# Four modulation vectors summed on VectorE, ScalarE and GpSimd during the projections, and a state-space term added by transposes

## The chip, the cores and the metric

One core of a Trainium2 chip runs the whole kernel. The metric is the device time of that core in microseconds (us), as the median of several runs. TensorE (PE in the profile) multiplies, VectorE (DVE), ScalarE (ACT) and GpSimd (POOL) do the elementwise work, SyncE (SP) issues most of the DMA transfers. Each engine takes its own instructions in order and waits on semaphores for the others.

## What is computed

Two transformer blocks in a row on 512 latent tokens of 1024 channels, with 256 context tokens. Cut to what the change touches:

```python
def first_block(x, c, ctx, c_ctx, w_mod, b_mod, ...):
    m_lat = jnp.split((silu(c) @ w_mod + b_mod)[:, None, :], 6, axis=-1)   # six vectors of 1024
    m_ctx = jnp.split(silu(c_ctx) @ w_mod + b_mod, 6, axis=-1)
    h_lat = modulate(rmsnorm(x, norm1_g), m_lat[0], m_lat[1])              # first shift and scale
    mix_lat = token_mixers(h_lat, h_ctx, w_in, ...)                        # projections, then four mixers
    x = x + m_lat[2] * (mix_lat @ w_out)
    h_lat = modulate(rmsnorm(x, norm2_g), m_lat[3], m_lat[4])              # second shift and scale
    return x + m_lat[5] * expert_choice_ffn(h_lat, ...)                    # 16 experts

def second_block(x, c, ctx, c_ctx, w_mod, b_mod, ...):
    sh1, sc1, gt1, sh2, sc2, gt2 = jnp.split(silu(c) @ w_mod + b_mod, 6)
    # state-space branch: per chunk, y = (masked decay * C B^T) xs  +  decay * C state  +  d * xs
    x = x + gt1 * token_mixer(modulate_2(x, norm1_g, sh1, sc1), ...)
    return x + gt2 * conv_ffn(modulate_2(x, norm2_g, sh2, sc2), ...)
```

The vectors of the change are number 3 and 4 of each block's six, `m_lat[3]`, `m_lat[4]`, `sh2` and `sc2`: only their latent row is needed, and only behind the mixers.

## The kernel before, in words

The program is written as Python generators, one for each strand of work, which `weave` (L321), `beside` (L360) and `filled` interleave: the strand with the least progress goes next, and each `yield` says how much progress it made. What is so interleaved goes to a scheduler that fixes the order of each engine's instructions by the order of writing and by when operands are ready; buffers come from rings and arenas, so a load into a ring's buffer waits for the last reader of that buffer. The stages in order of time are these.

- **Input** (0 to 52 us). `a_in` (L601) sums the first shift and scale of block one and makes the modulated tokens.
- **Projections** (52 to 222 us). `g_proj` (L701) multiplies the tokens with eleven blocks of `w_in` of 256 columns. A block comes in two loads of half a megabyte on SP (`base<-in_cola`), is split by `wsplit` (L1948) into a high part (ScalarE, L1963) and a low part (VectorE or GpSimd in turn, L1964), one block ahead, and multiplied in three passes by `chan` or `tok` (`bank_mm`, 24 matmuls to an accumulator, four accumulators). ScalarE and VectorE in turn copy the accumulators out (`cp`, L425 and L427). `a_gates` (L860) is a chain of small instructions on VectorE in the middle of it.
- **Mixers** (222 to 670 us). `phase_a` (L1443) weaves `g_dn`, a recurrence of twelve chunks in two directions (names `dn`, `bank_dn`, `bank_dnr`), with `others`: first `g_ft` and `g_na`, and beside them `g_mods`; then `g_df` beside `g_wo`; then `g_mid`.
- **Modulation vectors.** `g_mods` (L652) makes ten vectors for later. Each comes in two halves of 512 columns; `mod_rows` (L510) loads a half's weights in four loads of half a megabyte (a ring of three buffers, `mods<-in_cola`) and multiplies them by a 32-column silu vector, eight matmuls that leave rows. `mod_bcast` spreads the rows over 128 partitions by one more matmul, `mod_cols` (L521) turns them into columns by four transposes (L528), and `mod_cols_pk` (L533) packs them by eight matmuls into `bigbank`.
- **Router and experts** (670 to 1700 us), `g_b0`, `g_b1`, `g_b`.
- **Second block** (1700 us to the end). `part_c` weaves the attention `c_att` with `c_ssd`, the state-space branch, and then runs the output projections and the feed-forward part. In `c_ssd`, for each of four groups of eight heads, `state` (two directions, four steps) adds the term of the states into `of`, four chunks of 128 tokens by 512 channels. Then, for 16 pairs of a head pair and a chunk, `weights` builds the decay weights `W` (six VectorE instructions L2426 to L2430, two ScalarE steps and one of GpSimd, in a ring of four) and `mixed` adds two products into the accumulator `bank_y` (one bank): `xs` times `W`, and `of` times the identity, each for two heads of 64 channels. `out` reads the bank when its four chunks are done.

Of the kernel before, what the change touches and what calls it, by code (L numbers as in the profile page):

```python
# [390 lines left out]
class KA:  # L391
# [141 lines left out]
    def mod_cols_pk(self, s, wdram, bi, j, ring, rows, out):  # L533
        nc = self.nc
        t = self.big().rearrange("p (k g r) -> p k g r", k=8, g=4)
        for h in range(2):
            r = rows()
            self.mod_rows(s, wdram, 2 * j + h, ring, r)
            for kt in range(8):
                self.mm(t[64 * h:64 * h + 64, kt].rearrange("p g r -> p (g r)"), r[:, kt::8], self.ident)  # L540
        nc.vector.tensor_reduce(out, t[:, :, :, 0:2].rearrange("p c g r -> p c r g"), AX.X, OP.add)
        nc.vector.tensor_add(out, out, self.col("b_mod_pk", 8 * bi, 8)[:, :, None].to_broadcast([128, 8, 2]))
# [109 lines left out]
    def g_mods(self, tag, n):  # L652
        nc, I = self.nc, self.I
        self.md = tag
        with self.pool("mods") as P:
# [3 lines left out]
            self.mod_bcast(s1, wm, I["b_mod"], 2, wr, rows, self.gt1_b.ap(), self.sel)  # L659
# [5 lines left out]
            yield 0.1  # L665
            self.mod_bcast(s1, wm, I["b_mod"], 5, wr, rows, self.gt2_b.ap(), self.sel)
            yield 0.1
            mc, a = self.m2c_b.ap(), self.ab2_b.ap()
            s2, wm = self.s2b.ap(), "w_mod_2"
            for i, j in enumerate((0, 1, 3, 4)):  # L670
                self.mod_cols(s2, wm, "b_mod_2", j, wr, rows, mc[:, i])
                yield 0.1
            for i, (m, r, n) in enumerate(((1, 0, "norm1_g_2"), (1, 1, "norm1_g_2"), (3, 0, "norm2_g_2"))):
                nc.vector.scalar_tensor_tensor(a[:, i], mc[:, m, :, r], 1.0, self.col(n, 0, 8), op0=OP.add, op1=OP.mult)
            for i, j in enumerate((2, 5)):
# [8 lines left out]
                yield 0.1  # L684
# [16 lines left out]
    def g_proj(self, P):  # L701
# [91 lines left out]
        for t in range(4):  # L793
            z = nv()
            self.cp(z, self.tok(w, t))
            if t == 0:
                left()
            nc.scalar.dma_start(vdv[:, t], z)
        yield 0.04
        for t in range(2):  # L800
            self.cp(vc[:, t], self.tok(w, t, False))
        w.done()
# [4 lines left out]
        for i in range(2):  # L807
            nc.scalar.mul(q[:, i].rearrange("p (i r c) -> p r i c", i=4, r=8), self.chan(w, 128 * i).rearrange("p (r i c) -> p r i c", i=4, r=8), 0.125)
            yield 0.03
        w.done()  # L810
        w = block()
        for i in range(2):
            self.cp(k[:, i], self.chan(w, 128 * i), "v")
            if i == 0:
                next(gates)
                self.abT_b.free()
            self.cp(kc[:, i], self.chan(w, 128 * i, False))
            yield 0.05
# [6 lines left out]
        for a in range(2):  # L825
            w = block()
            for t in range(4):
# [4 lines left out]
                for e in range(2):  # L832
# [3 lines left out]
                    (nc.gpsimd.tensor_sub if e == 0 else nc.gpsimd.tensor_add)(o[:, :, :, e], o[:, :, :, e], u)  # L836
                yield 0.015
            if a == 1:
                for t in range(2):
                    self.cp(kc[:, t].rearrange("p m d -> p (m d)"), self.tok(w, t, False))  # L840
                yield 0.03
            w.done()
        w = block()
        for t in range(2):
            self.cp(v[:, t], self.tok(w, t, False))
        yield 0.03
        for t in range(4):
            self.cp(v[:, 2 + t], self.tok(w, t))
        yield 0.06
        w.done()  # L850
        w = block()
        for i in range(2):
            self.cp(self.uT_b.ap()[:, i], self.chan(w, 128 * i))
            yield 0.03
        w.done()
        cr.free()
        cr2.free()
# [896 lines left out]
class Kern(KB):  # L1754
# [517 lines left out]
    def c_ssd(self, P):  # L2272
# [84 lines left out]
        for gr in range(4):  # L2357
# [76 lines left out]
            def mixed(k):  # L2434
                pr, c = k // 4, k % 4
                if c == 0:
                    ys[pr] = self.bank((128, 512), "y")
                yb, W, tk = ys[pr], Ws.pop(k), slice(128 * c, 128 * c + 128)
                for z in range(2):
                    for h in range(2):  # L2440
                        o = 128 * pr + 64 * h
                        self.mm(yb[64 * h:64 * h + 64, tk], (of if z else xs)[:, c, o:o + 64], self.ident if z else W[:, h], z == 0, z == 1)
# [338 lines left out]
```

## Time and profile before

| | before |
|---|---|
| median of 3 runs | 2982.91 us (2982.39 to 2989.98) |
| the profiled execution | 2982.76 us |
| its span in the profile | 2980.9 us |
| TensorE busy | 2770.4 us, 93% of the span |
| VectorE, ScalarE, GpSimd busy | 1334.9, 902.3, 625.7 us |
| DMA moved | 658.53 MB, mean 221 GB/s |

How to read the profile: "busy" is the time in which an engine has at least one instruction under way. TensorE's instructions overlap at their ends, so the time that one takes in a stream is the distance of two starts and not its duration; a float32 matmul leaves two records, a transpose one. Names are those of the program's buffers without their numbers: `l`, `a`, `ab` and `base` are arenas of the first block, `sp` the ring of split weights, `mix` and `c` those of the second block.

### The profile page before, as it was taken

The numbers are of one execution on the slowest core, as the hardware profiler recorded it, in microseconds if no ns is written. First come the engines' busy times: TensorE is split into PE (matmuls) and PEld (weight loads), VectorE is DVE, ScalarE is ACT, GpSimd is POOL, SyncE is SP. The second block draws the span as 40 slices with busy tenths as digits, with TensorE's granted clock in tenths as the row PEclk, the third lists the DMA queues.
The fourth block names the chain that finished last, engine by engine and source line by source line (L and its number), as shares of the span: only waits on it lengthen the run. The fifth ranks groups of instructions, "written<-read, shape, count | busy, mean of one in ns | idle before, by whom it ended". The sixth has DMA issues, their size and how long they took to land.

```text
span 2980.9 us, 41808 instructions
## 1 busy us (share of the span) xinstructions
PE 2770.4 (93%) x16824; PEld 1776.0 (60%) x16824; DVE 1334.9 (45%) x2654; ACT 902.3 (30%) x1836; POOL 625.7 (21%) x660
## 2 busy tenths in 40 slices
PE   7999989997999999988888789999999899999998
PEld 4894547765334333332222267777777688888886
DVE  5522445655121211111101167878787854454445
ACT  5511225532111010100000044545454543343333
POOL 3121224531000000000000024232323322332222
PEclk9999999998999999999999999999999999999999
DMA  6216661038999999989999923324242464242331
GB/s 268 75 34 200 209 218 32 30 121 309 397 430 430 429 429 430 429 371 430 431 431 430 387 88 105 118 64 123 72 120 74 134 232 160 94 154 95 97 99 57
DMA packets 213122, 658.53 MB, mean 221 GB/s; under 512 B 13816, under 2 KB 131192, under 8 KB 188352
## 3 DMA queue, kind: packets, MB, share of 16 engines
q1 hardware_dynamic: 185504, 601.73, 52.4%
q10 hardware_dynamic: 26272, 49.93, 4.7%
q0 software_dynamic: 1152, 4.19, 0.3%
q8 instruction: 133, 2.18, 0.3%
q14 instruction: 61, 0.50, 0.1%
HBM read 632.07 MB, written 23.73 MB: 220 GB/s over the span
## 4 chain that ended last, share of the span: by engine, by line
PE 68%; DMA 16%; DVE 10%; issue 2%; ACT 2%; POOL 2%; SPq 1%; ACTq 0%; POOLq 0%; DVEq 0%
PE bank_mm L399 29%; PE bigbank L399 20%; DMA l<-in_w_up 6%; PE bank_pj L399 6%; DMA l<-in_w_down 4%; PE bank_c L399 4%; PE bank_dn L399 2%; DMA mods<-in_cola 2%; DMA l<-in_w_gate 1%; PE bank_sm L399 1%; DVE base L2426 1%; DVE mix L2430 1%; PE bank_dnr L399 1%; DVE mix L2429 1%; PE bank_mm L2181 1%
## 5 line engine op out<-in xcount | busy, mean ns | idle before, releaser
L399 PE MATMUL bank_pj<-c,c 128*128 128x512 f32 (+2 forms) x1368 | 319.7, 376 | 0.3 <-DVE c L1964 0.3
L399 PE MATMUL bank_mm<-c,c 128*128 128x512 f32 (+1 forms) x1608 | 304.4, 347 | 4.9 <-ACT b L1987 3.2
L399 PEld LDWEIGHTS bank_mm<-c,c 128*128 128x128 f32 x1608 | 259.3, 191 | 44.2 <-ACT b L1987 3.6
L399 PE MATMUL bigbank<-l 128*64 128x512 f32 (+1 forms) x1104 | 266.1, 594 | 17.9 <-DMA l<-in_w_up 13.1
L399 PEld LDWEIGHTS bank_pj<-c,c 128*128 128x128 f32 (+1 forms) x1368 | 225.7, 189 | 50.7 <-issue 17.5
L1963 ACT CAST c<-base 128x1024 fp32r<-128x1024 f32 x147 | 152.8, 1045 | 254.3 <-PE bigbank L399 105.7
L1964 POOL TENSOR_TENSOR c<-base,c 128x1024 fp32r<-128x1024 f32 x47 | 116.7, 2483 | 472.9 <-ACT c L1963 404.6
L1964 DVE TENSOR_TENSOR c<-base,c 128x1024 fp32r<-128x1024 f32 x100 | 136.3, 1365 | 136.8 <-ACT c L1963 133.7
L399 PEld LDWEIGHTS bigbank<-l 128*64 128x64 f32 (+1 forms) x1104 | 80.9, 141 | 175.8 <-issue 140.4
L1692 DVE TENSOR_TENSOR b<-l,bigbank 128x512 f32<-128x512 f32 x32 | 20.5, 683 | 340.8 <-PE bigbank L399 293.5
L1691 ACT ACTIVATE l<-bigbank 128x512 f32<-128x512 f32 x32 | 17.4, 595 | 423.7 <-PE bigbank L399 423.7
L399 PE MATMUL bank_mm<-l 128*64 128x512 f32 (+2 forms) x528 | 124.8, 601 | 9.1 <-DMA l<-in_w_down 8.0
L399 PE MATMUL bigbank<-out,c 128*128 128x512 f32 x480 | 113.8, 397 | 1.9 <-ACT out L2524 1.8
L399 PE MATMUL bank_c<-b 128*128 128x256 f32 (+3 forms) x496 | 110.0, 373 | 1.9 <-ACT b L425 0.8
L399 PE MATMUL bank_mm<-h,sp 128*128 128x512 f32 (+3 forms) x544 | 105.5, 382 | 4.3 <-ACT h L644 3.8
L399 PEld LDWEIGHTS bank_dn<-dn 64*64 64x64 f32 x1920 | 74.8, 134 | 55.0 <-issue 39.3
L399 PEld LDWEIGHTS bigbank<-out,c 128*128 128x128 f32 x480 | 91.7, 192 | 23.0 <-ACT out L2524 2.2
L399 PE MATMUL bigbank<-b,l 128*64 128x512 f32 x352 | 84.9, 614 | 21.8 <-DMA b<-in_w_up 10.9
L1717 DVE TENSOR_TENSOR b<-bank_mm,ab 64x512 f32<-64x512 f32 x16 | 10.9, 683 | 208.1 <-PE bank_mm L399 208.1
L1786 ACT ACTIVATE b<-bank_c,base 128x256 f32<-128x256 f32 x20 | 11.3, 563 | 304.6 <-PE bank_c L399 304.6
L399 PEld LDWEIGHTS bank_c<-b 128*128 128x128 f32 (+1 forms) x496 | 80.4, 188 | 37.2 <-issue 23.9
L399 PE MATMUL bigbank<-c,ffn 128*128 128x512 f32 x432 | 100.3, 390 | 0.0
(538 smaller groups left out, 5060.7 us busy)
## 6 DMA issues: line engine op xcount, KB each, us to landing
l<-in_w_up SPq DMA_DIRECT2D x36, 2048.0 KB, 14.6
l<-in_w_down SPq DMA_DIRECT2D x31, 2048.0 KB, 17.0
l<-in_w_gate SPq DMA_DIRECT2D x29, 2048.0 KB, 18.2
mods<-in_cola SPq DMA_DIRECT2D x80, 512.0 KB, 4.9
base<-in_w_in SPq DMA_DIRECT2D x68, 512.0 KB, 3.7
b<-in_w_gate SPq DMA_DIRECT2D x15, 2048.0 KB, 34.0
base<-in_w_gate SPq DMA_DIRECT2D x13, 2048.0 KB, 16.9
wo<-in_w_up SPq DMA_DIRECT2D x13, 2048.0 KB, 33.8
```

What stands on the lines that cost most here:

```text
L399: self.mm_ins = self.nc.tensor.matmul(out, l, r, start=start, stop=stop).ins
L1691: nc.scalar.activation(s, ac[0][:, j], AF.Silu)
L1692: nc.vector.tensor_mul(hid[:, 512 * j:512 * j + 512], s, ac[1][:, j])
L1717: nc.vector.tensor_mul(Y[pp, 0:512], dn[0:64], gt2[0:64, 0:512])
L1786: nc.scalar.activation(y, b, AF.Identity, scale=wc(1), bias=self.col(bname, i))
L1963: nc.scalar.copy(hi, raw)
L1964: (nc.vector if self.wn % 4 in self.losplit else nc.gpsimd).tensor_sub(lo, raw, hi.bitcast(F32))
L2181: nc.tensor.transpose(tb[:, z], p[:, 128 * (g0 + z):128 * (g0 + z) + 128], self.ident)
L2426: nc.vector.scalar_tensor_tensor(E[:, h], rw[:, h, 0], gc(1, 0, h), E[:, h], op0=OP.subtract, op1=OP.min)
L2429: nc.vector.tensor_scalar(W[:, h], cb[:, c, 0], gc(0, 0, h), None, op0=OP.mult)
L2430: nc.vector.scalar_tensor_tensor(W[:, h], cb[:, c, 1], gc(0, 1, h), W[:, h], op0=OP.mult, op1=OP.add)
```

## The change

Three things change.

1. `g_mods` makes six vectors where it made ten. The four that are left out, number 3 and 4 of both blocks, are made by the new `g_late_mods` inside `g_proj`, from the block behind the recurrence's query projections on to the last. Each half's weights now come in eight loads of a quarter megabyte (a ring of four buffers); VectorE (five of eight), ScalarE (three of eight, added by GpSimd) multiply them by the silu value of their partition and add up, and GpSimd adds the two sums (`mod_sums`). One half later TensorE sums over the partitions by matmuls with one moving column of ones (`mod_close`: eight of 64 columns for the packed form, four of 128 for the other), and VectorE adds the bias.
2. In `g_mods` the `yield` values change from a tenth to a sixth, so that the six vectors spread over the same stretch.
3. In `mixed` the product of `of` with the identity, two for each chunk, gives way to four transposes of 128 by 128 for each head pair, written into `bank_y` in front of the first product.

```diff
-    def mod_cols_pk(self, s, wdram, bi, j, ring, rows, out):
-        ...
+    def mod_sums(self, s, wdram, j, rings):
+        nc, (wr, da, pa, pp) = self.nc, rings
+        wv = self.block(wdram, j)
+        d, o = da(), pa()
+        for kt in range(8):
+            w, c = wr(), s[:, kt, 0:1]
+            self.ld(w, wv[:, kt])
+            if kt == 0:
+                nc.vector.tensor_scalar(d, w, c, None, op0=OP.mult)
+            elif kt in (1, 3, 6):
+                z = o if kt == 1 else pp()
+                nc.scalar.activation(z, w, AF.Copy, scale=c)
+                if kt > 1:
+                    nc.gpsimd.tensor_add(o, o, z)
+            else:
+                nc.vector.scalar_tensor_tensor(d, w, c, d, op0=OP.mult, op1=OP.add)
+            if kt == 3:
+                yield
+        nc.gpsimd.tensor_add(o, o, d)
+        self.msum = o
+
+    def mod_close(self, o, h, bias, out, pk):
+        p, n = (slice(64 * h, 64 * h + 64), slice(0, 8)) if pk else (slice(0, 128), slice(4 * h, 4 * h + 4))
+        t = self.bank((128, 8), "md")
+        for c in range(8 if pk else 4):
+            self.mm(t[p, n.start + c:n.start + c + 1], o[:, c::8] if pk else o[:, c * 128:(c + 1) * 128], self.km("one", 1))
+        self.nc.vector.tensor_add(out[p, n], t[p, n], bias[p, n])
+
+    def g_late_mods(self, P):
+        ...
+        of = [Ring(P, [512], 2, more=[Buf(self.M, [512]) for _ in range(2)])] + [Ring(self.M, [512], n) for n in (1, 2, 1)]
+        ...
+            for h in range(2):
+                yield from self.mod_sums(s, w, 2 * j + h, of)
+                if owed:
+                    owed.pop()()
+                owed.append(lambda o=self.msum, h=h, n=n, name=name, out=out, pk=pk: self.mod_close(o, h, self.col(name, n, 8), out, pk))
+                yield
+        owed.pop()()
@@ g_mods
-            self.mod_cols_pk(s1, wm, 0, 3, wr, rows, mp[:, 0])
-            yield 0.1
-            self.mod_cols_pk(s1, wm, 1, 4, wr, rows, mp[:, 1])
-            for i, j in enumerate((0, 1, 3, 4)):
-                self.mod_cols(s2, wm, "b_mod_2", j, wr, rows, mc[:, i])
-                yield 0.1
+            for j in range(2):
+                self.mod_cols(s2, wm, "b_mod_2", j, wr, rows, mc[:, j])
+                yield 1 / 6
@@ g_proj, at some 16 places from the block of the values on
+            if t % 2 == 0:
+                next(sums)
@@ c_ssd, mixed
                 if c == 0:
-                    ys[pr] = self.bank((128, 512), "y")
+                    b = ys[pr] = self.bank((128, 512), "y")
+                    for z in range(4):
+                        nc.tensor.matmul(b[:, 128 * z:128 * z + 128], of[:, z, 128 * pr:128 * pr + 128], self.ident, start=z == 0, stop=False, is_transpose=True)
-                for z in range(2):
-                    for h in range(2):
-                        o = 128 * pr + 64 * h
-                        self.mm(yb[64 * h:64 * h + 64, tk], (of if z else xs)[:, c, o:o + 64], self.ident if z else W[:, h], z == 0, z == 1)
+                for h in range(2):
+                    o = 128 * pr + 64 * h
+                    self.mm(yb[64 * h:64 * h + 64, tk], xs[:, c, o:o + 64], W[:, h], False, c == 3)
```

Where instructions stand in an engine's row, before and after, is told by the built programs. SP's row in the projections of the kernel before, from the weights of the first blocks (`base_95`) to the first loads of the mixers (`dn` and `mods`):

```order
L430 DMA base_95<-in_cola 128x1024 x4
L430 DMA ab_138<-in_b_mod 128x1024
L430 DMA ab_139<-in_b_mod 128x1024
L430 DMA base_95<-in_cola 128x1024 x16
L430 DMA dn_1853<-in_k_ct 128x2x512 x2
L430 DMA mods_1951<-in_cola 128x1024
```

The same of the kernel after; the loads of the sums are those of 128x512 into `sp_920`, `sp_921` and two pieces of `l_105`:

```order
L430 DMA base_95<-in_cola 128x1024 x10
L430 DMA l_105<-in_cola 128x512 x2
L430 DMA sp_921<-in_cola 128x512
L430 DMA l_105<-in_cola 128x512
L430 DMA sp_920<-in_cola 128x512
L430 DMA l_105<-in_cola 128x512
L430 DMA base_95<-in_cola 128x1024
L430 DMA l_105<-in_cola 128x512 x2
```

Sixteen weight loads in a row have become ten, and the last six stand one by one among the loads of the sums.

VectorE's row of the kernel before, in the block of the values and at the head of the chain of `a_gates` (L874 on); L427 copies an accumulator out and L1964 is a low part of split weights:

```order
L427 COPY sp_888<-bank_mm 128x256
L1964 TENSOR_TENSOR sp_353<-base_95,sp_349 128x1024
L427 COPY l_105<-bank_mm 128x256
L874 TENSOR_TENSOR l_105<-bank_mm,ab_123 128x48
L587 SCALAR_TENSOR_TENSOR l_105<-l_105 128x48
```

And of the kernel after, where the same lines are L2013 (split), L923 and L624 (`a_gates`), and L541 and L548 are the sums:

```order
L541 TENSOR_SCALAR l_105<-l_105,ab_126 128x512
L548 SCALAR_TENSOR_TENSOR l_105<-sp_920,ab_126,l_105 128x512
L2013 TENSOR_TENSOR sp_353<-base_95,sp_349 128x1024
L548 SCALAR_TENSOR_TENSOR l_105<-l_105,ab_126 128x512
L427 COPY l_105<-bank_mm 128x256
L548 SCALAR_TENSOR_TENSOR l_105<-l_105,ab_126 128x512
L923 TENSOR_TENSOR l_105<-bank_mm,ab_123 128x48
L548 SCALAR_TENSOR_TENSOR l_105<-sp_921,ab_126,l_105 128x512
```

The sums stand in front of the low part of the weights and of the copies, one or two at a time.

TensorE's row in the second block of the kernel before, where the first head pair of a group fills `bank_y`; `base_59` is the identity, `mix_9896` is `of`, `mix_9895` is `xs`, the others are `W` (the first product of the pair stands 74 rows further ahead):

```order
L399 MATMUL bank_y<-base_59,mix_9896 64x128 x2
L399 MATMUL bank_y<-mix_9903,mix_9895 64x128 x2
L399 MATMUL bank_y<-base_59,mix_9896 64x128 x2
L399 MATMUL bank_y<-mix_9904,mix_9895 64x128 x2
L399 MATMUL bank_y<-base_59,mix_9896 64x128 x2
L399 MATMUL bank_y<-mix_9905,mix_9895 64x128 x2
```

And of the kernel after, where `mix_9938` is `of` and `mix_9937` is `xs`:

```order
L2488 MATMUL bank_y<-base_59,mix_9938 128x128 x4
L399 MATMUL bank_y<-mix_9944,mix_9937 64x128 x2
L399 MATMUL bank_y<-mix_9945,mix_9937 64x128 x2
L399 MATMUL bank_y<-mix_9946,mix_9937 64x128 x2
L399 MATMUL bank_y<-mix_9947,mix_9937 64x128 x2
```

Four transposes stand ahead of all products of the head pair, and no product stands ahead of them any more.

## Rows read from the trace of the kernel before

**Rows 1.** The page's chain that ended last, shares of the span by engine.
```profile
PE 68%; DMA 16%; DVE 10%; issue 2%; ACT 2%; POOL 2%; SPq 1%; ACTq 0%; POOLq 0%; DVEq 0%
```

**Rows 2.** Stages: length, busy PE PEld DVE ACT POOL (counts), clock, DMA share, GB/s.
```profile
122.00:222.00 100.00, 100.00 (x821) 93.75 (x820) 25.09 (x78) 20.76 (x36) 21.70 (x27) 1.00 0.12 42
...
240.00:320.00 80.00, 74.38 (x699) 40.27 (x697) 29.37 (x67) 16.47 (x50) 16.72 (x25) 1.00 0.61 196
320.00:400.00 80.00, 74.64 (x807) 39.90 (x806) 38.46 (x100) 23.81 (x74) 17.34 (x28) 1.00 0.68 215
400.00:452.00 52.00, 46.22 (x535) 24.78 (x536) 22.58 (x54) 13.89 (x44) 11.54 (x18) 1.00 0.62 198
452.00:520.00 68.00, 67.12 (x849) 50.80 (x847) 40.53 (x97) 39.11 (x110) 34.02 (x62) 1.00 0.11 33
...
745.00:1700.00 955.00, 871.44 (x3726) 324.81 (x3724) 142.13 (x261) 77.22 (x158) 30.70 (x30) 0.99 0.99 423
```

**Rows 3.** Instructions on the tile `mods`: count, duration ns min/median/max, first and last start.
```profile
L399 PE MATMUL bank_mm<-mods,ab x336: 589/592/697, 245.2 to 452.1; 128*32 128x512 f32 x160, 128*128 128x512 f32 x8
L430 SPq DMA_DIRECT2D mods<-in_cola x80: 327/328/1096, 220.2 to 444.3; - x80
...
L399 PE MATMUL bigbank<-base,mods x64: 283/283/387, 271.6 to 307.5; 128*64 128x128 f32 x64
...
L528 PE MATMUL bank_mm<-base,mods x32: 272/273/328, 338.5 to 409.2; 128*128 128x128 f32 x32
```

**Rows 4.** Waits, 222 to 670 us: who waited for whom, total, times, longest.
```profile
PE bank_mm L399 <- DMA mods<-in_cola: 11.2, 15, 2.1
```

**Rows 5.** TensorE in order of time, mixers: start us, duration us, what.
```profile
261.80 2.11 PE L399 MATMUL bank_mm<-mods,ab 128*128 128x512 f32 x6
...
264.56 1.05 PE L399 MATMUL bank_mm<-mods,ab 128*32 128x512 f32 x4
265.54 0.32 PE L399 MATMUL bank_dn<-dn 64*64 64x64 f32 x2
...
271.65 2.19 PE L399 MATMUL bigbank<-base,mods 128*64 128x128 f32 x16
```

**Rows 6.** Busy time of the instructions on `mods` alone, three stretches.
```profile
240.00:320.00 80.00, 37.42 (x182) 12.93 (x182) 2.75 (x4) 1.76 (x3) 1.00 0.61 196
320.00:400.00 80.00, 33.80 (x159) 7.55 (x158) 2.07 (x3) 2.92 (x5) 1.00 0.68 215
400.00:460.00 60.00, 22.43 (x92) 4.33 (x92) 4.77 (x7) 1.17 (x2) 1.00 0.57 181
```

**Rows 7.** Groups of instructions, 104 to 222 us: shapes, count, busy us, mean ns.
```profile
L399 PE MATMUL bank_mm<-base,l 128*64 128x4 f32 x96 | 3.0, 199 | 0.0
...
L399 PE MATMUL bank_mm<-l,a 128*128 128x24 f32 x8 | 1.0, 258 | 0.0
```

**Rows 8.** VectorE and GpSimd in order of time, around 105 and 111 us.
```profile
105.69 0.69 DVE L732 SCALAR_TENSOR_TENSOR l<-l 128x512 f32<-128x512 f32 x1
...
111.11 2.45 DVE L734 SCALAR_TENSOR_TENSOR l<-l 128x512 f32<-128x512 f32 x1 [1.40 <-ACT l L730]
...
110.63 2.39 POOL L1964 TENSOR_TENSOR sp<-base,sp 128x1024 fp32r<-128x1024 f32 x1 [8.48 <-ACT sp L1963]
```

**Rows 9.** State-space stage: records on `bank_y`, starts of matmuls and transposes, one stretch.
```profile
L399 PE MATMUL bank_y<-base,mix x256: 272/273/474, 1866.8 to 2364.5; 128*64 128x128 f32 x128
...
1872.57 0.39 PE L399 MATMUL bank_y<-mix,mix 128*64 128x128 f32 x4
1872.79 0.39 PE L399 MATMUL bank_y<-base,mix 128*64 128x128 f32 x4
...
1881.29 0.66 PE L2181 MATMUL bank_mm<-base,mix 128*128 128x128 f32 x4
1881.71 2.48 PE L399 MATMUL bank_pj<-c,c 128*128 128x512 f32 x14
...
1880.00:1900.00 20.00, 19.64 (x189) 17.05 (x187) 19.41 (x55) 13.89 (x35) 8.55 (x8) 1.00 0.43 127
```

More of the change, by code (lines that the diff above doesn't have):

```diff
@@ new lines, in mod_close @@
+    def mod_close(self, o, h, bias, out, pk):
[5 more added lines that the diff above has]
+    def g_late_mods(self, P):
+        s1, s2 = self.s1b.ap(), self.s2b.ap()
+        mp, mc = self.mpk_b.ap(), self.m2c_b.ap()
+        of = [Ring(P, [512], 2, more=[Buf(self.M, [512]) for _ in range(2)])] + [Ring(self.M, [512], n) for n in (1, 2, 1)]
+        owed = []
+        for s, w, j, name, n, out, pk in ((s1, "w_mod", 3, "b_mod_pk", 0, mp[:, 0, :, 0], True), (s1, "w_mod", 4, "b_mod_pk", 8, mp[:, 1, :, 0], True),
+                                          (s2, "w_mod_2", 3, "b_mod_2", 24, mc[:, 2, :, 0], False), (s2, "w_mod_2", 4, "b_mod_2", 32, mc[:, 3, :, 0], False)):
+            for h in range(2):
[5 more added lines that the diff above has]
+        owed.pop()()
+        for z in of:
+            for b in z.b:
+                b.free()
@@ L797, in g_proj @@
                 left()
+                cr.free()
+                cr2.free()
+                sums = self.g_late_mods(P)
+            if t % 2 == 0:
+                next(sums)
             nc.scalar.dma_start(vdv[:, t], z)
@@ L801, in g_proj @@
             self.cp(vc[:, t], self.tok(w, t, False))
+        next(sums)
         w.done()
@@ L808, in g_proj @@
             nc.scalar.mul(q[:, i].rearrange("p (i r c) -> p r i c", i=4, r=8), self.chan(w, 128 * i).rearrange("p (r i c) -> p r i c", i=4, r=8), 0.125)
+            next(sums)
             yield 0.03
@@ L816, in g_proj @@
                 self.abT_b.free()
+                next(sums)
             self.cp(kc[:, i], self.chan(w, 128 * i, False))
+            next(sums)
             yield 0.05
@@ L836, in g_proj @@
                     (nc.gpsimd.tensor_sub if e == 0 else nc.gpsimd.tensor_add)(o[:, :, :, e], o[:, :, :, e], u)
+                if t % 2 == 0:
+                    next(sums)
                 yield 0.015
@@ L840, in g_proj @@
                     self.cp(kc[:, t].rearrange("p m d -> p (m d)"), self.tok(w, t, False))
+                next(sums)
                 yield 0.03
@@ L845, in g_proj @@
             self.cp(v[:, t], self.tok(w, t, False))
+        next(sums)
         yield 0.03
@@ L848, in g_proj @@
             self.cp(v[:, 2 + t], self.tok(w, t))
+            if t == 1:
+                next(sums)
         yield 0.06
@@ L853, in g_proj @@
             self.cp(self.uT_b.ap()[:, i], self.chan(w, 128 * i))
+            if i == 0:
+                next(sums)
             yield 0.03
         w.done()
-        cr.free()
-        cr2.free()
+        for _ in sums:
+            pass
     def a_gates(self):
```

19 lines of the change are left out of this document (4 added, 15 removed).

## The prediction

> **What bounds the kernel now.** I read the page's chain first, then the busy times by stage, then the waits and the order in time of the stages that the diff touches. The chain that ended last is TensorE for 68% and DMA for 16% [rows 1]. The stages differ [rows 2]. In the projections (122 to 222 us) TensorE is busy for the whole 100 us and the DMA engines for 0.12. In the mixers with the modulation vectors (240 to 452 us) TensorE is busy 195 of 212 us, and the DMA share is 0.61 to 0.68. Behind that the mixers go on without modulation vectors (452 to 520 us), TensorE busy 67 of 68 us. The experts (745 to 1700 us) are held by DMA, 0.99 busy at 423 GB/s; their weights begin to stream when the mixers end, so whatever shortens the mixers moves that whole block forward, one for one. TensorE is thus the place to save in the first 670 us, and the change takes work from it in one stage and adds a little in another.
>
> **Part 1, four vectors leave the mixer stage.** The vectors shown as `mods` cost TensorE 37.42 + 33.80 + 22.43 = 93.7 us busy there [rows 6], in 336 records of rows times weights (16 of them spread a row over 128 partitions), 64 of packing and 32 transposes [rows 3]; a float32 matmul leaves two records, a transpose one. Packing is 2.19 / 16 = 0.137 us a record, so 8.8 us. The 16 spreading records are what remains of a piece of six beside a piece of four, (2.11 - 1.05) / 2 = 0.53 us each, 8.5 us [rows 5]. A transpose of 128x128 follows the next at 0.42 / 4 = 0.105 us [rows 9], so 3.4 us. The other 320 records keep 73.0 us, 0.228 each. Ends overlap: a piece of four lasts 1.05 us but the next starts 0.98 us behind it [rows 5], which leaves 0.213 us of TensorE's order. Four of ten vectors go: 8 halves x 16 records = 128 x 0.213 = 27.2 us, all packing 8.8 us, half of the transposes 16 x 0.105 = 1.7 us. Sum **-37.7 us**.
>
> With them go 32 of the 80 half-megabyte loads [rows 3]. TensorE waited 11.2 us on those loads [rows 4]; 32 / 80 of it is 4.5 us, and the 48 left are spread over the same other work with the same three buffers, so more may vanish: between 0 and 11.2, I take **-6 us**. Thinner TensorE work exposes more of the recurrence's chain (matmul, copy, matmul). The stretch at 452 us bounds this: 849 records in 68 us, 12.5 per us, at 99% busy [rows 2]. At 240 to 452 us there are 699 + 807 + 535 = 2041 records; without the 208 removed and in some 170 us it is 10.8 per us, less dense than what already runs without loss. Between 0 and 8 us, I take **+3 us**.
>
> **Part 2, the same vectors in the projections.** TensorE gets 32 column sums of 64 columns and 16 of 128, each with one moving column, 64 and 32 records. No row shows this form. The nearest are 96 records of 64-column weights with four moving columns in 3.0 us, 0.031 each, and 8 of 128-column weights with 24 moving columns in 1.0 us, 0.125 each [rows 7]. Low end 64 x 0.031 + 32 x 0.062 = 4; high end, 64 x 0.1 + 32 x 0.125 = 10.4. I take the two rows as they are, 2 + 4 = **+6 us**, all on the path, since TensorE is full there.
>
> The sums themselves should lie beside TensorE. VectorE gets 40 instructions of 512 elements at the 0.69 us of the same form [rows 8], at most 27.6 us; GpSimd 24 adds at half of 2.39 us [rows 8], 28.8 us; ScalarE 24 scalings, some 0.6 us each by VectorE's row, 15 us. In 122 to 222 us VectorE is busy 25.1 us, ScalarE 20.8, GpSimd 21.7 [rows 2]. SP gets 64 loads of 256 KB: 16.8 MB over 90 us is 186 GB/s more, beside 42 GB/s now. The order shows them in front of the last six weight loads of the projections; each such load can wait for a buffer that a sum frees. Those weights are not needed for more than one block of 10 us or longer, so a few us of delay on SP cost nothing. In VectorE's row the sums stand between copies out of the accumulators. A sum that waits for its load holds the copy behind it, and that holds TensorE when four accumulators are full. 821 records in 100 us are 0.122 us each [rows 2], an accumulator takes 24, 2.9 us, so three ahead give 8.8 us of cover; a half's work on both engines is 56.4 / 8 = 7.0 us. That is close, so I don't cost it at nothing: 0 to 16 us (next paragraph), **+4 us**.
>
> What can eat that cover is seen in one pair of rows: an instruction of VectorE with two SBUF inputs that takes 0.69 us lasted 2.45 us from 111.11 us, while GpSimd ran from 110.63 for 2.39 us [rows 8]; it ended just behind GpSimd. If none of the new work overlapped, VectorE and GpSimd together would need 25.1 + 27.6 + 21.7 + 28.8 = 103 us, and the sums have only 122 to about 210 us, 88 us. The excess, 15 to 16 us, is the upper end above and a rival below. The Trainium skill says the same of that pair (page "SBUF — State Buffer", section "SBUF: two separate sides"): VectorE and GpSimd share one port pair as an exclusive lock, held for a whole instruction, which counts for VectorE instructions with two SBUF inputs. It speaks against putting a sum on both engines at once; by it the projections would come out some 16 us longer, and the trace's 2.45 us agrees.
>
> **Part 3, the state-space term.** 128 matmuls against the identity go, 256 records [rows 9], four of which follow one another in 0.22 us: 14.1 us. 64 transposes of 128x128 come, at 0.105 us 6.7 us. On TensorE alone that is -7.4 us. But where they stand VectorE is the fuller engine, 19.41 of 20 us against TensorE's 19.64 of overlapped busy time [rows 9], and it builds the weights for these matmuls. A new wait comes too: the first product of each head pair now stands behind the transposes, which need all four chunks, so its weight buffer is freed later in each of four groups. A build is six VectorE instructions; 55 in 19.41 us are 0.35 us each, 2.1 us a build, at most 8.5 us in all. Between -7.4 and +8.5, I take **-2 us**.
>
> **Sum.** The profiled execution took 2982.76 us (span 2980.9), 0.15 below the median of the runs, so no shift is needed. 2982.8 - 37.7 - 6 + 3 + 6 + 4 - 2 = **2950 us**, 1.1% faster.
>
> **Rivals.**
> *The sums fill VectorE and GpSimd.* The pair of rows above speaks for it; against it, some of VectorE's work reads the accumulators and can overlap. The +4 becomes +16: 2962 us.
> *The recurrence binds.* The mixers can't run faster than the chain between TensorE and the other engines, and half of the 43.7 us stays behind as waits on copies: 2972 us. The denser stretch at 452 us speaks against it.
> *Slower.* VectorE holds the accumulators in each half, so that the sums are not hidden at all and their 56.4 us stand in the path of the projections in place of the 4: 3002 us. It takes a half that keeps VectorE's copies back by more than the 8.8 us of cover, each time; the load waits added to 7.0 us could do it.
> *The state-space edit costs.* With +8.5 in place of -2: 2960 us. And the case that the vectors' load leaves the mixers without their end moving, because the weights of the experts start by another release, would give 2983; the chain speaks against it.
>
> **How the numbers follow.** Forecast, within some 10 us: 0.60. Sums fill the engines 0.14, recurrence binds 0.10, state-space edit costs 0.05, end doesn't move 0.04, slower 0.07. The range reaches down to every good end together (-37.7 - 11.2 + 4 - 7.4: 2930) and up past the recurrence's case, 2974. About 0.3% (9 us) is what a measurement of this kernel can tell from no change, so faster means under 2974: nearly all of the first four cases, 0.86; same 0.07; slower 0.07.
>
> **What would show it.** In the profile after: 48 loads of `mods`, TensorE's records of `mods` down from 432 to 224; the same work end (now 452 us) some 30 us earlier, and the experts' stretch of full DMA too. The projections should still show TensorE full, ending 6 to 12 us later; waits of TensorE on VectorE, GpSimd or their accumulators there, in sum over 15 us, would prove the second or the slower rival. Waits on copies of the recurrence over 10 us in the mixers would prove the third. In the second block `bank_y` should show 256 records plus 64 transposes, and the stage at most 7 us shorter.

## The result, and the profile after

The changed kernel took 2955.7 us (median of 4 runs, 2953.3 to 2957.9) against 2985.2 for the kernel before in the same runs: ratio 0.9899, 95% interval 0.9882 to 0.9917, 1.0% faster. The forecast was 2950 us, with a range of 2930 to 2974. The profiled execution took 2957.9 us, its span 2956.1.

The chain of the page has the same shape as in [rows 1]:

```profile
PE 67%; DMA 16%; DVE 10%; issue 2%; POOL 2%; ACT 2%; SPq 0%; ACTq 0%; POOLq 0%; DVEq 0%
```

The stages, with the columns of [rows 2]. The projections now run to 238.4 us in place of 219.1, and the mixers with modulation vectors end at 421 us in place of 452:

```profile
122.00:240.00 118.00, 117.90 (x905) 110.40 (x905) 64.82 (x128) 35.49 (x59) 59.72 (x49) 0.94 0.52 173
240.00:320.00 80.00, 77.93 (x647) 39.23 (x641) 29.98 (x65) 20.26 (x63) 17.91 (x35) 1.00 0.57 184
320.00:400.00 80.00, 78.67 (x926) 46.31 (x928) 43.33 (x108) 24.76 (x80) 23.96 (x41) 1.00 0.49 157
400.00:430.00 30.00, 28.60 (x314) 16.48 (x310) 14.91 (x37) 8.41 (x26) 5.81 (x9) 1.00 0.42 132
...
720.00:1675.00 955.00, 868.45 (x3720) 322.98 (x3718) 142.18 (x261) 76.92 (x157) 30.70 (x30) 0.99 0.99 422
```

To see where the time went I took marks, the starts of records that both kernels have: the first record on `bank_dn` (the projections are over), the last of the recurrence on `bank_dn`, the first on `bank_c`, the last of the experts on it, the last state-space product, the last of `ffn`.

| us | before | after | difference |
|---|---|---|---|
| projections over | 219.1 | 238.4 | +19.3 |
| last of the recurrence | 665.5 | 640.6 | -24.9 |
| first of `bank_c` | 707.0 | 682.0 | -25.0 |
| last of `bank_c` | 1296.5 | 1272.5 | -24.0 |
| last state-space product | 2364.5 | 2340.3 | -24.2 |
| last of `ffn` | 2971.0 | 2945.9 | -25.1 |

The rows of the first two marks, before (last start of the first row, first start of the second) and after:

```profile
L399 PE MATMUL bank_dn<-dn x1920: 218/218/366, 254.5 to 665.5; 64*64 64x64 f32 x192
...
L399 PE MATMUL bank_dn<-a,l x192: 218/218/268, 219.1 to 489.9; 64*64 64x64 f32 x192
```

```profile
L399 PE MATMUL bank_dn<-dn x1920: 218/218/366, 276.0 to 640.6; 64*64 64x64 f32 x192
...
L399 PE MATMUL bank_dn<-a,l x192: 218/218/267, 238.4 to 463.9; 64*64 64x64 f32 x192
```

All is decided by 665 us: the mixers are 44.2 us shorter (446.4 to 402.2), the projections 19.3 longer, and behind that nothing moves, the state-space stage included. -44.2 + 19.3 is -24.9, the whole difference of the two profiled executions.

**The mixers.** The rows on `mods` that answer to [rows 3], and TensorE's wait on these loads from 240 to 430 us, which was 11.2 us in [rows 4]:

```profile
L399 PE MATMUL bank_mm<-mods,ab x208: 592/592/697, 264.3 to 420.6; 128*32 128x512 f32 x96, 128*128 128x512 f32 x8
L430 SPq DMA_DIRECT2D mods<-in_cola x48: 327/328/459, 238.7 to 413.2; - x48
...
L528 PE MATMUL bank_mm<-base,mods x16: 272/273/329, 322.5 to 358.8; 128*128 128x128 f32 x16
```

```profile
PE bank_mm L399 <- DMA mods<-in_cola: 2.9, 6, 0.8
```

208 + 16 records in place of 432, 48 loads in place of 80.

**The projections.** No wait of TensorE stands in the trace there (0.1 us idle in 116), and yet they are 19.3 us longer. Two things fill them: the closes, as I call the matmuls of `mod_close` that end a vector's half, and a lower clock. TensorE in order of time, around the first close (the 16 records of 128x1) and around one of the 128-column ones:

```profile
133.99 7.35 PE L399 MATMUL bank_mm<-h,sp 128*128 128x512 f32 x24
141.28 2.08 PE L399 MATMUL bank_md<-base,l 128*64 128x1 f32 x16
143.29 11.17 PE L399 MATMUL bank_mm<-h,sp 128*128 128x512 f32 x48
...
197.56 0.95 PE L399 MATMUL bank_md<-base,l 128*128 128x1 f32 x8
198.37 14.64 PE L399 MATMUL bank_mm<-sp,h 128*128 128x256 f32 x120
```

From start to start a 64-column close takes 2.01 us, 0.126 a record, a 128-column one 0.81, 0.10 a record; all eight together take 8.1 + 3.3 = 11.4 us. And the granted clock, 1.00 throughout before [rows 2], falls to 0.50, the lower of its two levels (1.2 of 2.4 GHz), in four stretches. Four windows of 4 us (the clock is the third number from the end):

```profile
130.00:134.00 4.00, 4.00 (x107) 3.85 (x105) 2.19 (x3) 2.60 (x3) 1.28 (x1) 1.00 0.69 254
134.00:138.00 4.00, 4.00 (x14) 3.17 (x12) 4.00 (x4) 0.72 (x1) 3.96 (x2) 0.57 0.77 253
...
154.00:158.00 4.00, 4.00 (x33) 3.87 (x32) 3.69 (x3) 1.67 (x5) 3.48 (x3) 1.00 0.42 155
158.00:162.00 4.00, 4.00 (x22) 3.92 (x21) 1.44 (x6) 0.59 (x4) 0.78 (x1) 0.57 0.81 267
```

The window at 134 us shows 14 records, where the same window of the kernel before, at a clock of 1.00, shows 19. The first stretch begins behind the gates' 96 records with four moving columns, the other three behind 64-column closes (those at 155, 170 and 182 us). Behind the 64-column close at 141 us and the four of 128 columns no stretch begins. Summing 1 minus the clock over windows of 1 us gives 6.8 us lost. 11.4 + 6.8, and 0.5 us that the stage already began later, are 18.7 of the 19.3.

So at this point the reading was: closes and clock. The experiments showed that this is half of it.

### The profile page after: what moved, and what is told of

Its sections match the earlier page's. It is cut to its first block, busy times and chain, and to the rows that moved or that the text cites. A ratio compares the mean times of both kernels' runs of the same rounds, so it can differ in the third digit from the quotient of the medians.

```text
span 2956.1 us, 41376 instructions
## 1 busy us (share of the span) xinstructions
PE 2750.2 (93%) x16520; PEld 1770.8 (60%) x16520; DVE 1371.3 (46%) x2688; ACT 915.3 (31%) x1856; POOL 659.5 (22%) x684
## 4 chain that ended last, share of the span: by engine, by line
PE 67%; DMA 16%; DVE 10%; issue 2%; POOL 2%; ACT 2%; SPq 0%; ACTq 0%; POOLq 0%; DVEq 0%
PE bank_mm L399 26%; PE bigbank L399 21%; PE bank_pj L399 7%; DMA l<-in_w_up 5%; DMA l<-in_w_down 5%; PE bank_c L399 4%; PE bank_dn L399 3%; DMA l<-in_w_gate 1%; PE bank_sm L399 1%; DMA mods<-in_cola 1%; DVE mix L2478 1%; PE bank_mm L2230 1%; DVE base L2475 1%; PE bank_dn L1042 1%; DVE mix L2479 1%
## 5 line engine op out<-in xcount | busy, mean ns | idle before, releaser
L2013 POOL TENSOR_TENSOR c<-base,c 128x1024 fp32r<-128x1024 f32 x47 | 116.0, 2469 | 479.7 <-ACT c L2012 421.3
L2013 DVE TENSOR_TENSOR c<-base,c 128x1024 fp32r<-128x1024 f32 x100 | 135.9, 1363 | 135.9 <-ACT c L2012 132.7
L1740 ACT ACTIVATE l<-bigbank 128x512 f32<-128x512 f32 x32 | 17.4, 595 | 426.0 <-PE bigbank L399 426.0
L399 PEld LDWEIGHTS bank_mm<-h,sp 128*128 128x128 f32 (+1 forms) x544 | 85.5, 187 | 25.4 <-ACT h L681 4.0
```

The lines of the kernel that those rows point to most:

```text
L399: self.mm_ins = self.nc.tensor.matmul(out, l, r, start=start, stop=stop).ins
L1740: nc.scalar.activation(s, ac[0][:, j], AF.Silu)
L2013: (nc.vector if self.wn % 4 in self.losplit else nc.gpsimd).tensor_sub(lo, raw, hi.bitcast(F32))
```

## The experiments

**What ends the projections.** Theory A: the closes and the clock behind them. Theory B: the sums on VectorE and GpSimd. First the closes alone are left out:

```
-        for c in range(8 if pk else 4):
-            self.mm(t[p, ...], o[:, c::8] if pk else o[:, ...], self.km("one", 1))
-        self.nc.vector.tensor_add(out[p, n], t[p, n], bias[p, n])
+        self.nc.vector.tensor_copy(out[p, n], bias[p, n])
```

> The changed kernel without the 48 column-sum matmuls that end the four moved vectors (their 96 records); the vectors are then the bias alone, every load and every sum stays. In the changed kernel the projections ended 19.3 us later than before (238.4 against 219.1 us) and TensorE had no wait in them. Theory A, the closes and the clock behind them: the closes take 11.4 us of TensorE's order and the stretches at the granted clock of 0.5 to 0.65 cost some 6.8 us more, so the projections end near 220 us and the whole run takes about 2938 to 2940 us. Theory B, the sums on VectorE and GpSimd stretch the projections in a way the waits do not show: the projections still end past 230 us and the run takes 2946 us or more. The clock: by A no stretch under 0.9 is left between 140 and 220 us.

Measured: 2958.6 us (2 runs), the projections over at 238.4 us, to the tenth where they were. Theory A fell. The row of the first mark, TensorE's waits from 122 to 240 us, and two windows of it:

```profile
L399 PE MATMUL bank_dn<-a,l x192: 218/218/267, 238.4 to 467.5; 64*64 64x64 f32 x192
```

```profile
PE bank_mm L399 <- DVE l L873: 8.8, 4, 3.4
PE bank_mm L399 <- DVE l L427: 1.1, 1, 1.1
PE bank_mm L399 <- ACT l L544: 0.4, 1, 0.4
```

```profile
178.00:182.00 4.00, 0.61 (x4) 0.44 (x4) 1.81 (x6) 0.03 (x1) 3.00 (x4) 0.86 0.50 154
182.00:186.00 4.00, 4.00 (x20) 4.00 (x20) 3.16 (x11) 0.69 (x1) 3.51 (x4) 0.50 0.90 281
```

With the closes gone, 10.3 us of waits came up, 8.8 of them on the rotary multiplies (L873), VectorE's readers of the accumulators, and the clock fell around two such waits as well as behind the gates; 8.1 us of TensorE's busy time were lost by it. So 238.4 is where VectorE's lane and the clock together end the stage; no run shows that lane at a clock of 1.00 throughout. The mirror image, sums left out and closes kept:

```
-            w, c = wr(), s[:, kt, 0:1]
+            w = o if kt == 0 else wr()
             self.ld(w, wv[:, kt])
-            if kt == 0:
-                nc.vector.tensor_scalar(d, w, c, None, op0=OP.mult)
...
-        nc.gpsimd.tensor_add(o, o, d)
```

> The changed kernel with all loads and all closes, but without the products and sums on VectorE, ScalarE and GpSimd: each column sum goes over the first of the eight loaded tiles, so the four vectors are wrong. Theory A (closes and clock): the projections end where those of the changed kernel do, 236 to 240 us, the clock falls again behind the 64-column closes, and the run takes 2952 to 2958 us. Theory B (VectorE and GpSimd hold TensorE up): the projections end 8 us earlier or more, and the run takes 2947 us or less.

Measured: 2953.5 us (2 runs), the projections over at 236.2 us, no wait of TensorE, the clock at half in three stretches (5.1 us lost), none of them behind the gates:

```profile
L399 PE MATMUL bank_dn<-a,l x192: 218/218/267, 236.2 to 461.2; 64*64 64x64 f32 x192
```

By its bounds this is theory A's case. So there are two limits side by side: closes and clock end the stage at 236 without the sums, VectorE's lane at 238.4 without the closes. Taking away either buys 2.2 us at most. The loads were all there in this run and no wait came of them, so they alone are not a third limit. Another close, with all the sums in place, shows the same:

```
-            self.mm(t[p, ...], o[:, c::8] if pk else o[:, ...], self.km("one", 1))
+                self.nc.tensor.transpose(t[:, c % 4], o[:, c::8] if pk else o[:, c * 128:(c + 1) * 128], self.ident)
+            self.nc.vector.tensor_reduce(out[:, 4 * q:4 * q + 4], t, AX.X, OP.add)
```

> The changed kernel with another close: per vector eight transposes of 128x128 and two reductions on VectorE in place of 16 matmuls of 64 columns or 8 of 128 with one moving column; the half sums of a vector lie side by side, and a scaled tile is written over its load. Theory A: 32 transposes at 0.105 us are 3.4 us in place of 11.4, and with 128 moving columns the clock does not fall behind them, so the projections end 8 to 15 us earlier, near 225 to 230 us, and the run takes 2941 to 2948 us, faster than both kernels. Theory B: no change within 3 us, 2953 to 2958 us, since the sums set the end.

Measured: 2956.4 us (4 runs, 2956.0 to 2958.5), ratio to before 0.9916, 0.9899 to 0.9933; over at 238.4. The 32 transposes took 3.9 us of TensorE's order, no stretch of lower clock stood behind any of them, one only behind the gates (3.4 us lost), and TensorE stood idle for 10.2 us instead, 10.0 of them in waits on VectorE. Theory B again. The price of this close is on VectorE: eight reductions of 0.68 us.

**What holds VectorE.** It was busy only 64.8 of 118 us in the changed kernel, so it is not full; it waits in its order. Its waits there (122 to 240 us):

```profile
DVE l L541 <- POOL l L551: 14.9, 6, 3.5
DVE l L548 <- DMA l<-in_cola: 11.0, 8, 2.5
```

One such wait in order of time, VectorE first, then GpSimd:

```profile
174.83 1.66 DVE L548 SCALAR_TENSOR_TENSOR l<-sp,ab,l 128x512 f32<-128x512 f32 x1
176.41 0.15 DVE L560 TENSOR_TENSOR ab<-bank_md,ab 64x8 f32<-64x8 f32 x1
180.03 0.49 DVE L541 TENSOR_SCALAR l<-l,ab 128x512 f32<-128x512 f32 x1 [3.47 <-POOL l L551]
...
181.22 0.28 DVE L875 TENSOR_TENSOR sp<-bank_mm,sp 128x128 f32<-128x128 f32 x1
```

```profile
175.89 2.86 POOL L2013 TENSOR_TENSOR sp<-base,sp 128x1024 fp32r<-128x1024 f32 x1
178.71 1.29 POOL L551 TENSOR_TENSOR l<-l 128x512 f32<-128x512 f32 x1
```

A half's partial sum `d` is done; GpSimd has still to split a weight tile (2.86 us) before it adds `d` to the other partial sum (L551), and only then may VectorE start the next half, since `d` has one buffer. The rotary multiply that frees an accumulator (L875) stands behind it. Leaving out that last addition, closes left out too:

```
-        nc.gpsimd.tensor_add(o, o, d)
```

> The changed kernel without the 96 records of the closes (as x1_no_closes) and also without the eight last additions on GpSimd, which join the two partial sums of a half; the four vectors are the bias alone. Without closes TensorE waited 10.3 us on VectorE in the projections, and VectorE had waited 15.5 us on those eight additions, since the next half's partial sum reuses the buffer that they read. Theory A, VectorE's lane holds TensorE and that one buffer is what holds VectorE: the waits of TensorE between 122 and 240 us fall from 10.3 to under 4, the projections end near 228 to 232 us in place of 238.4. Theory B, the loads or the pairing with GpSimd hold VectorE: the waits stay over 7 us and the end stays past 235.

Measured: 2948.2 us (2 runs), over at 230.1 us. TensorE's waits went from 10.3 to 5.7 us and the time lost to the clock from 8.1 to 3.4, in a stage that began 1 us later. The end is the one of theory A; the waits stayed above its 4 us, and VectorE still waited 16 us on loads. So the buffer, with the eight additions that also leave GpSimd, is worth some 5 us of waits; that the clock's other 5 us went because of it is not shown, since the clock differs between executions too. An attempt to give that addition more time without new memory, with the close of x3_transposes:

```
-            if kt == 0:
+            if kt == 1:
                 nc.vector.tensor_scalar(d, w, c, None, op0=OP.mult)
-            elif kt in (1, 3, 6):
+            elif kt in (0, 2, 5):
```

> As x3_transposes (closes by transposes), but the first load of a half goes to ScalarE and the second to VectorE, so that the eight additions on GpSimd have one load more of time before VectorE needs their buffer. In x3_transposes TensorE waited 9.5 us on VectorE's multiplies of the rotary part, and VectorE 8.3 us on those additions and 17.4 us on loads. Theory A (the buffer): the projections end at 230 to 235 us and the run takes 2947 to 2953 us. Theory B (the loads, or the pairing with GpSimd): the end stays within 2 us of 238 and the run at 2954 to 2958 us.

Measured: 2957.1 us (4 runs, 2953.4 to 2961.6), over at 237.2. Against x3_transposes VectorE's wait on the addition went from 8.3 to 1.1 us and its waits on loads grew from 17.4 to 23.3: one wait took the other's place. What did help changes four things at once on top of that close (the partial sum in an accumulator bank, other loads for ScalarE, the last addition on VectorE, five buffers for the loads in place of four), so that their shares are not told apart:

```
-        d = da()
+        d = self.bank((128, 512), "ss")
...
-            elif kt in (1, 3, 6):
+            elif kt in (0, 2, 4):
...
-        nc.gpsimd.tensor_add(o, o, d)
+        nc.vector.tensor_add(o, o, d)
```

> As x3_transposes, but VectorE's partial sum stands in an accumulator bank in place of a buffer of SBUF, VectorE makes the last addition itself, ScalarE and GpSimd take loads 0, 2 and 4, and the loads have five buffers. VectorE's multiply-add then has one input from SBUF; the 40 in the changed kernel took 0.74 us at the least and 2.86 at the most, mean about 1. Theory A, the sums on VectorE and GpSimd (the wait for the joined buffer and the lengthened instructions) set the end once the closes are cheap: the multiply-adds stay near 0.75 us, TensorE's waits in the projections fall below 4 us, they end at 225 to 231 us, and the run takes 2943 to 2949 us, faster than the changed kernel by 7 to 13. Theory B, the loads hold VectorE: the end stays past 235 us and the run at 2952 us or more.

Measured: 2949.3 us (4 runs, 2945.9 to 2957.1), over at 230.2, TensorE's waits 2.3 us, the end and the waits as theory A had them; the profile is that of the fastest run. VectorE's multiply-adds, grouped from 122 to 240 us, in the changed kernel (two rows) and here (two rows, under a fence of their own; count, busy us, mean ns):

```profile
L548 DVE SCALAR_TENSOR_TENSOR l<-l,ab 128x512 f32<-128x512 f32 x16 | 16.6, 1035 | 11.1 <-DMA l<-in_cola 11.0
L548 DVE SCALAR_TENSOR_TENSOR l<-sp,ab,l 128x512 f32<-128x512 f32 x16 | 14.5, 906 | 2.7 <-DMA sp<-in_cola 2.5
```

```profile
L548 DVE SCALAR_TENSOR_TENSOR bank_ss<-l,ab,bank_ss 128x512 f32<-128x512 f32 x19 | 14.3, 753 | 6.6 <-DMA l<-in_cola 6.1
L548 DVE SCALAR_TENSOR_TENSOR bank_ss<-sp,ab,bank_ss 128x512 f32<-128x512 f32 x13 | 9.7, 748 | 4.5 <-DMA sp<-in_cola 4.4
```

With one input in an accumulator bank the form takes 0.75 us on average and 0.76 at most; with both in SBUF it took 0.97 on average and 2.86 at most. The Trainium skill (page "SBUF — State Buffer", section "SBUF: two separate sides") names VectorE instructions with two SBUF inputs, beside those in a 2-port mode, as the ones that share a lock with GpSimd; these rows agree.

**The clock.** What was left in that kernel were two stretches of lower clock, 5.1 us in all: one behind the gates' piece, one behind a wait of 1.8 us with small pieces following it. The gates' 96 records were put in four pieces between products, the first of them earlier than the one piece had stood:

```
             for d in range(2):
...
+            if n % 3 == 2:
+                yield
```

> The changed kernel itself once more, as the measure beside z1_spread_gates on the same chip: 2953 to 2958 us, the projections ending near 238 us, with three or four stretches at half the granted clock between 130 and 190 us that cost some 6.8 us.

> As y6_psum_sum (closes by transposes, VectorE's partial sums in an accumulator bank), and the 96 gate records with four moving columns, which stood in one piece of 3.4 us before a stretch of 6.6 us at half the granted clock, stand in four pieces of 24 between the projections' products. y6_psum_sum ended the projections at 230.2 us and took 2949.3 us, 2945.9 to 2957.1. Theory A, the clock falls behind a piece of TensorE work with few moving columns: the stretch near 134 us goes, the projections end 2 to 4 us earlier, at 226 to 229 us, and the run takes 2942 to 2948 us, 8 to 13 us under the changed kernel in the same rounds. Theory B, the clock falls for another reason: the same 3 to 6 us are lost, the projections end at 230 to 232, the run takes 2946 to 2951.

Measured in the same rounds: the changed kernel 2958.9 us (5 runs, 2955.1 to 2962.8), ratio to before 0.9924 (0.9910 to 0.9937); the new one 2949.9 (4 runs, 2947.3 to 2951.3), 0.9891 (0.9875 to 0.9906): 9.0 us less, and faster than both kernels. The projections are over at 228.9 us. Its windows from 122 us on show a clock of 1.00 in all:

```profile
122.00:140.00 18.00, 18.00 (x159) 16.33 (x159) 10.81 (x21) 8.38 (x14) 4.98 (x3) 1.00 0.60 191
140.00:180.00 40.00, 39.25 (x263) 36.14 (x262) 29.86 (x57) 13.29 (x25) 17.13 (x12) 1.00 0.80 264
180.00:229.00 49.00, 45.82 (x337) 43.11 (x337) 28.92 (x63) 11.93 (x18) 20.61 (x26) 1.00 0.39 127
```

The 72 records behind the gates' place show what it is worth, first with the gates in one piece (y6_psum_sum), then with them spread:

```profile
134.28 19.31 PE L399 MATMUL bank_mm<-h,sp 128*128 128x512 f32 x72
```

```profile
134.95 16.51 PE L399 MATMUL bank_mm<-h,sp 128*128 128x512 f32 x72
```

So the clock and the end went as theory A said. The cause is likely but not shown: this is one profile, and behind the one piece of gates the clock fell in eight of the other twelve, and stayed at 1.00 in the kernel before, x2_no_sums, x4_old_ssd and y4_half_build. The end gained 1.3 us only, since waits on VectorE took some of it back (3.9 us in place of 2.3), and the run stands some 2 us above the 2942 to 2948 of theory A, inside the range of theory B. Its ratio to before, 0.9891, is that of y6_psum_sum, 0.9895, so the spread by itself bought no time that the runs can tell. Against the first measurement of the changed kernel, 2955.7, the new one is 5.8 us less and not 9.0. The changed kernel run again lost 3.4 us to the clock in two stretches, where its first profile had lost 6.8 in four, and its projections were over at 238.6 all the same. Its stage had begun 1.2 us later (the gates at 132.25 us against 131.09), and TensorE waited 1.6 us on VectorE. Where the clock falls thus differs from one execution to the next, and waits on VectorE take up part of the difference.

**The mis-sized close.**

```
+            r = slice(64 * a, 64 * a + 64) if pk else p      # a = (c + h) % 2
-            self.mm(t[p, n.start + c:n.start + c + 1], ...
+            self.mm(t[r, n.start + c:n.start + c + 1], ...
```

> The changed kernel with its 64-column closes issued to the two halves of TensorE's columns in turn (even sums to rows 0 to 63, odd ones to 64 to 127) in place of one half for a whole piece, so that sums land in rows that are not theirs and the two packed vectors are wrong. It tests the term that was mis-sized: 0.031 us a record was taken from the gates' records, which alternate, and 0.126 was measured where all sixteen go to one half. Theory A, alternation is the difference: 16 records take 0.5 to 1.1 us in place of 2.02. Theory B, the single moving column or the strided weights are: 1.9 to 2.1 us again. By either the run takes 2952 to 2958 us, since VectorE's lane ends the projections near 238 us as well.

Measured, the same close as above:

```profile
140.79 1.13 PE L399 MATMUL bank_md<-base,l 128*64 128x1 f32 x16
141.85 11.18 PE L399 MATMUL bank_mm<-h,sp 128*128 128x512 f32 x48
```

1.06 us from start to start, 0.066 a record: of the difference of 0.095 between 0.126 and 0.031 alternation takes away 0.060, and 0.035 stays, with the strided weights or the single column as its cause, not told apart. The run took 2956.4 us (2 runs), over at 236.1, with only 1.7 us lost to the clock and 5.5 us of waits in the place of what the closes gave back.

**The state-space sums.** The changed kernel with the old sums:

```
-                        nc.tensor.matmul(b[:, 128 * z:128 * z + 128], of[...], self.ident, ..., is_transpose=True)
+                        self.mm(yb[...], (of if z else xs)[:, c, o:o + 64], self.ident if z else W[:, h], z == 0, z == 1)
```

> The changed kernel with the state-space sums as they were: 256 records of products with the identity in place of 64 transposes. The first transposes of that stage came at 1843.2 us and the last record at 2340.3, 497.1 us, against 497.7 before. Theory A, the edit is worth nothing, since VectorE and the new wait of the transposes for their chunks take the place of the 7.4 us of TensorE: 2954 to 2958 us. Theory B, it is worth its 7 us and something else in the stage lost as much: 2961 to 2964 us.

Measured: 2956.4 us (4 runs, 2952.6 to 2957.4). From the last record of the experts to the last state-space product it took 1066.8 us, with the edit 1067.8 (1069.1 in the second run of the changed kernel), before 1068.0: the edit is worth nothing within 2 us. The eight other profiles with the edit and full builds lie between 1065.3 and 1069.7. Its 64 transposes are there, and so is a wait:

```profile
L399 PE MATMUL bank_y<-mix,mix x256: 272/273/476, 1843.8 to 2340.3; 128*64 128x128 f32 x128
...
L2488 PE MATMUL bank_y<-base,mix x64: 270/273/475, 1843.2 to 2334.1; 128*128 128x128 f32 x64
```

```profile
PE bank_y L2488 <- DVE base L2498: 4.6, 5, 2.5
```

L2498 is VectorE's reader of the one `bank_y`; the transposes come first into the bank and wait for it, and the products then wait for their weights (GpSimd's L2480, 3.2 us). Is VectorE's building of the weights the pace?

```
-                    nc.vector.scalar_tensor_tensor(W[:, h], cb[:, c, 1], gc(0, 1, h), W[:, h], op0=OP.mult, op1=OP.add)
```

> The changed kernel without the second of the two weighted terms in each build of the state-space weights in the second block (128 instructions of VectorE left out, two of six in a build, some 0.3 us each, about 40 us of VectorE), so the state-space sums are wrong. Theory A, VectorE's builds and not TensorE set the pace of that stage, which is why 7 us less of TensorE bought nothing: from the last record of the expert stage (1272.5 us in the changed kernel) to the last state-space product (2340.3) it takes 1067.8 us, and now 8 to 25 us less; the run takes 2931 to 2948 us. Theory B, TensorE or the loads set it: less than 3 us, 2953 to 2957 us.

Measured: 2954.2 us (2 runs); the same stretch took 1059.2 us, 8.6 less, the low edge of theory A. The whole run's time is in theory B's range: its profile shows 4.2 us of the 8.6 at the end, because the experts were done 1.8 us later and the part behind the last state-space product took 2.6 us longer than in the changed kernel. The 46 us of VectorE's work that went bought 8.6, where 7.4 us of TensorE's bought none: VectorE's lane has a part in the pace, and by the small yield it is not the only one. Which other wait takes over is open.

## Why the prediction was right, and where its steps were not

**The end and the sign held, with some luck.** 2950 was forecast, 2955.7 measured, 2957.9 in the profiled execution. Against the sum the projections came out 9.3 us worse (19.3 in place of 6 and 4), the state-space edit 2 worse and the mixers 3.5 better; that the last error went the other way is luck.

**Four vectors leave** (-37.7, waits -6, recurrence +3, together -40.7): measured -44.2. TensorE's busy time on `mods` from 240 to 460 us fell by 36.0 us (93.7 to 57.7), the load waits by 8.3, more than the 6 taken; that is the whole of it. In the denser stretch behind (430 to 580 us) TensorE was idle for 7.4 us against 5.9 in the like stretch before (452 to 602), so the recurrence did not bind; that rival is out.

**The closes** (+6): 11.4. The failed step is the row: 0.031 us a record was read from the gates' records in [rows 7], which go to the two column halves in turn, while a packed close sends all sixteen to one half. It measured 0.126, above even the 0.1 of the upper bound, and 0.066 with the halves in turn. The 128-column term, 0.125, measured 0.10.

**The clock** had no term. Stretches at half clock cost 6.8 us in the profiled execution and 3.4 in that of the second run.

**The stall through the sums** (+4, 0 to 16): TensorE's waits were 0.1 us, so that row for row the term came out too high, and the sign that was to prove it (waits over 15 us) stayed away. The mechanism was there none the less: the rival "the sums fill VectorE and GpSimd" priced it at 16 us, and with the sums but no closes TensorE waits 10.3 us, loses 8.1 to the clock and ends the stage 19.3 us later than before. What failed is that I added the terms. Closes and clock (to 236 us) and VectorE's lane (to 238.4, the clock's loss with it) run beside each other, and the stage takes the longer. The work was also more than my rows gave: VectorE's 40 instructions took 39.4 us and not 27.6, GpSimd's 24 additions 33.9 and not 28.8. Still the engines were not full, as the cause that I worked out would have had them: VectorE was busy 65 of 118 us and held up by one buffer that GpSimd reads, and by loads. The pair of rows on which that rival stood [rows 8] shows the lengthened multiply-adds, by estimate 7 us of VectorE (32 times 0.97 less 0.75), beside 14.9 us of waits on the buffer; what each costs the stage is not told apart.

**The state-space edit** (-2, -7.4 to +8.5): 0 within 2 us, inside the bounds. Both reasons given there have a row: the transposes' new wait was 4.6 us, and 46 us less work on VectorE, the fuller engine, did shorten the stage, by 8.6.

**The rest** moved one for one with the mixers' end, as the first part said: the experts' stretch stands 25.0 us earlier with the same 0.99 of DMA.

## What to carry to other kernels

When work moves under a full engine, ask of each engine separately where the stage would end if the others cost nothing; the stage takes the latest of these, so terms from different engines are not added, and taking away the one that the trace shows may buy nothing. An engine that is half idle can still be the limit: look at what its in-order queue waits for (here a single buffer shared with a slower engine) and at what stands behind that wait. A column sum takes less of TensorE as transposes with a reduction on VectorE than as matmuls with one moving column, 3.5 to 3.9 us against 11.4 here; VectorE pays 5.2 us for it, and where VectorE's lane ends the stage, as in x3_transposes, nothing is gained.

## What the runs showed that I had not expected

TensorE's granted clock fell to half while TensorE had no wait at all (0.1 us idle in 116), behind pieces of 16 to 96 records with one or four moving columns, while no fall began behind a piece of 8 transposes alone; with the one kind of piece replaced and the other spread it stayed at 1.00, in one profile. It fell around waits of 1.8 to 3.4 us too, though not around each (none behind one of 2.6 us in x1_no_closes). Nor did it fall behind each such piece: the same 96 gate records in one piece were followed by a clock of 1.00 in four kernels, the one before among them. Why, and why one kernel loses 3.4 us in one execution and 6.8 in another, is open.

A matmul record with 64 columns of weights and one moving column follows the next after 0.126 us when all go to one half of the columns, 0.066 when the halves alternate; with 128 columns it is 0.10.
